# Attention without dividing the softmax: the sums go through DRAM into the gate, and three smaller moves

## The chip, the core and the metric

The kernel runs on one core of a Trainium2 chip. A core has TensorE (PE: matrix products, with a weight load, PEld, before each), VectorE (DVE), ScalarE (ACT) and GpSimd (POOL), which run their own instruction queues and wait for each other by semaphores, and SyncE (SP), which here only issues DMAs. Operands lie in on-chip memory of 128 partitions; products land in eight PSUM banks. The metric is the time on the device in microseconds, the median of several executions. Everything is float32; a product in full precision is made of three products of values that are split into a rounded high part and a low rest ("fp32r").

## The reference

Two layers; the change lies in the token mixer of the first, a forgetting attention over 1024 positions, 16 heads of 64:

```
proj = h @ w_in
q, k, v, o, fl = jnp.split(proj, [D, 2 * D, 3 * D, 4 * D], axis=-1)
q = rmsnorm(q.reshape(B, S, H, Dh), q_gain)
k = rmsnorm(k.reshape(B, S, H, Dh), k_gain)
logf = jax.nn.log_sigmoid((fl + b_f).astype(jnp.float32))
F = jnp.cumsum(logf, axis=1).transpose(0, 2, 1)
...
    logits = jnp.einsum('bqhd,bkhd->bhqk', q[:, q0:q1], k[:, :q1]).astype(jnp.float32) * scale
    decay = F[:, :, q0:q1, None] - F[:, :, None, :q1]
    logits = jnp.where(kpos <= qpos, logits + decay, -jnp.inf)
    p = jax.nn.softmax(logits, axis=-1).astype(v.dtype)
    outs.append(jnp.einsum('bhqk,bkhd->bqhd', p, v[:, :q1]))
att = jnp.concatenate(outs, axis=1).reshape(B, S, D)
return (att * jax.nn.sigmoid(o)) @ w_out
```

Before it stand `h = modulate(rmsnorm(x, norm1_g), shift, scale)` and the conditioning that gives shift and scale; after it a gated MLP with a convolution, then a second layer with a spatial-gating MLP and another gated MLP. The division in the softmax is by one number per query and head, so it may be made before the product with v, after it, or on the gate sigmoid(o), which the product is multiplied with.

## The kernel before

**Order.** The kernel is traced in the order of its code. A planner then draws the order of each engine at build time from a simulated timeline: an instruction that was traced earlier goes first, but one whose inputs are ready in that simulation may pass one that waits. SP's queue is ordered in the same way. In the attention part only a few orders are fixed by hand (`chain`); TensorE's order there is the planner's. A buffer ring hands a buffer out again when all that used it is done.

**Start (`fox`, L445 to L502).** Eight tiles of x are loaded; `square` sums each row on ScalarE, `rstd` makes the factors with some thirteen small operations on VectorE, for the tiles 0 and 1, 2 and 3, 4 to 7 together. `ada_first(q)` (L413) makes a quarter of shift and scale from two pieces of weights of 1 MB, multiplied and added on VectorE (L429, L431). `raw_pieces` (L403) says in which buffers the eight pieces lie: qq, w, kh, kl, w, pt, qq, w; the ring w has two slots, and qq, kh and kl are the buffers that hold q and k later. `norm_t` normalizes (L465), transposes on TensorE (L157) and copies to h (L471); the loop after it applies scale and shift on ScalarE (L492), rounds (L493) and subtracts (L119). The weights of the first three gate products (`o_weights(…, True)`, buffers qkv) are rounded on ScalarE (L126), and their low parts are made on POOL (L119).

**Gate products.** `o_proj(p)` computes o for a head pair, and `o_out` stores its sigmoid to the DRAM tile nso. Pairs 0 to 2 are computed at the start, pairs 3 to 7 in a loop with `o_proj` and a conditioning job each, after the projection of pair 0 (`proj`) and `forget`, which makes the sums F (fq on chip, nf in DRAM).

**Attention.** Eight head pairs p. `proj(p)` (matmuls pj) makes q, k and v of a pair in two halves of 512 positions, normalizes q and k per head (L590 to L598), and is the filler: `tick` lets some of its matmuls follow each score tile. `heads_qk(rw, half)` transposes q and k of a half (ps qk, L157), scales and rounds them on ScalarE into qq and kh (L697), makes the low parts on VectorE (L699) and copies kh once more (L703). The rows of kl that belong to the other head are zero; POOL writes them once (L686), 16 instructions. `scores(p, fb, qt)` does the query tile qt of 128 for both heads: POOL makes the decay row F[t]-F[s] and masks it (L738, L742), TensorE the products s, VectorE adds the two and takes the minimum (L762), ScalarE the exponent with its sum (L773), VectorE the reciprocal of the sum (L775); then the row is scaled by it, for head 0 on ScalarE (L777), for head 1 on VectorE (L779). `values(p, g, hd, v)` takes 256 queries g of one head: transposes of the probabilities (ms, L157), a copy (L797) and a low part (L119 pt), products pv with v; at the end the two halves of the product are added to av, and after head 1 VectorE multiplies the gate with it (L816), so, which was loaded from nso; the result goes to nat in DRAM (L818), for pair 7 to the chip. The output product (op) of the last stage reads nat and w_out.

The loop over pairs traces: value product of the last pair, v, `scores` 1, the end of this pair's projection (`until`), `heads_qk` of half 1, `scores` 2, value product (0, head 0), `scores` 3, value product (0, head 1), the second half of v, `scores` 4, and so on; near its end it prepares half 0 of the next pair. For pair 0 half 0 is prepared at L981, right before `scores` 0. Score tiles 0 to 3 need half 0 alone.

Of the kernel before, what the change touches and what calls it, by code (L numbers as in the profile page):

```python
# [8 lines left out]
F32 = mybir.dt.float32  # L9
# [58 lines left out]
class Trunk:  # L68
# [278 lines left out]
    def fox(self):  # L347
# [4 lines left out]
        nso = self.tile(self.dram, [8, P, S], F32, "nso")  # L352
        nf = self.tile(self.dram, [H, S], F32, "nf")
        self.xd = self.tile(self.dram, [4, 2, P, S], F32, "xd")
        h = {}
        c = self.const

        with ExitStack() as es:
# [44 lines left out]
            def raw_pieces():  # L403

                nm = ("qq", "w", "kh", "kl", "w", "pt", "qq", "w")[len(pieces)]
                pieces.append(nm)
                if nm == "pt":
                    return [T([P, 2, 2, 256], F32, "pt", 3) for _ in range(2)]
                return [self.wslot([P, 4, 2, 256], F32) if nm == "w" else T([P, 4, 2, 256], F32, nm, 1)]

# [41 lines left out]
            rs = []  # L452
            for st0, n in ((0, 2), (2, 2), (4, 4)):
                ss = self.tile(self.small, [P, 4], F32, "n_ss")
                for i in range(n):
                    j = self.square(ss, i, xn[st0 + i], self.hslot(F32).rearrange("p a f -> p (a f)"))
                    if st0 + i == 0:
                        self.chain("act", j)
                r = self.rstd(ss, n)
                rs += [r[:, i : i + 1] for i in range(n)]  # L460
# [223 lines left out]
            for hd in range(2):  # L684
                for c in range(0, S, P):
                    nc.gpsimd.tensor_scalar(  # L686
                        KL[hd][own[1 - hd], c : c + P], self.ones[own[1 - hd]], 0.0, None, op0=ALU.mult
                    )

# [41 lines left out]
            def scores(p, fb, qt):  # L731
# [22 lines left out]
                for j, (c0, c1) in enumerate(zip(cuts, cuts[1:])):  # L754
# [10 lines left out]
                    tick(n / P)  # L765
                    flush()
                for hd in range(2):
                    d = st_t[hd, qt][:, :nk]
                    nm = sm[hd][:, 0:1]
                    if nk > 512:  # L770
                        nc.vector.tensor_tensor(nm, nm, sm[hd][:, 1:2], op=ALU.min)
                    l = self.tile(self.small, [P, 1], F32, "ll")
                    nc.scalar.activation(d, d, AF.Exp, bias=nm, scale=-1.0, accum_out=l)  # L773
                    r = self.tile(self.small, [P, 1], F32, "lr")
                    nc.vector.reciprocal(r, l)  # L775
                    if hd == 0:
                        nc.scalar.activation(d, d, AF.Copy, scale=r)  # L777
                    else:
                        nc.vector.tensor_scalar(d, d, r, None, op0=ALU.mult)  # L779

            def values(p, g, hd, v):

                if hd == 0:
# [6 lines left out]
                for kt in range(0, 2 * g + 2, 2):  # L790
                    last = kt == 2 * g
                    blocks = [(kt, 2 * g), (kt, 2 * g + 1)]
                    blocks += [(kt + 1, 2 * g + 1)] if last else [(kt + 1, 2 * g), (kt + 1, 2 * g + 1)]
                    nb = len(blocks) * P
                    ps = self.transpose4([st_t[hd, qt][:, j * P : (j + 1) * P] for j, qt in blocks])
                    pt = T([P, 2, 512], F32R, "pt", 3)
# [45 lines left out]
            for p in range(PO, 8):  # L842
                o_proj(p)
                self.run_jobs(jobs, 1, u4)


# [133 lines left out]
            fb = f_rows(0)  # L980
            heads_qk(rws[0], 0)  # L981
            scores(0, fb, 0)
            v0 = None
            for p in range(8):
# [5 lines left out]
                until(p, 1)  # L990
                heads_qk(rws[p], 1)
                scores(p, fb, 2)
                values(p, 0, 0, v)
                scores(p, fb, 3)
                values(p, 0, 1, v)
# [1000 lines left out]
```

## Time and profile before

| | |
|---|---|
| median of 3 runs | 2636.36 us (2635.47 to 2638.59) |
| the profiled execution | 2637.63 us; its span 2635.8 |
| mean granted clock of TensorE | 0.988 |
| TensorE busy | 2552.9 us, 97% of the span |
| VectorE, ScalarE busy | 2074.0 us (79%), 1461.9 us (55%) |
| POOL busy | 183.7 us, all before 720 us |
| TensorE's chain that ended last | 86% of the span |

The span runs from the first to the last instruction. A row of the timeline gives the start, the duration, engine, line, operation, tiles (out<-in), shapes and, in brackets, the idle time before it and what ended it; ACTq or SPq is an engine's queue, which here issues DMAs. "PE s L104 <- ACT kh L703" means that a matmul of the scores waited for ScalarE's copy of kh at L703. PEclk is the share of full speed that TensorE was granted. Most matmuls are recorded under the helper's L104, transposes under L157, rounding under L126 and low parts under L119, so their tiles tell them apart: o (gate), pj (projection), s (scores), pv (values), op (output), ms (transposes and small sums).

### The profile page before, as it was taken

Reading aid. Unit: us, or ns where it says so; the run is one execution under the profiler, and the core shown is the slowest. Engines: PE = TensorE matmul, PEld = TensorE weight load, DVE = VectorE, ACT = ScalarE, POOL = GpSimd, SP = SyncE. Lnnn points to the kernel's source line nnn. Section 1 sums busy time; section 2 is a strip of 40 time slices with the busy share of each in tenths; the row PEclk is TensorE's granted clock in tenths of the full one; section 3 lists DMA queues with packets and bytes.
Section 4 is the critical chain, followed back from the end, with each engine's and each line's share of the span. In section 5 each row is a group of like instructions: output and inputs, shape, how many; then the busy total and the mean of one; then the engine's idle time right before and its main releaser. Section 6 shows DMA issues by size and latency. Waiting matters only on the chain.

```text
span 2635.8 us, 35388 instructions
## 1 busy us (share of the span) xinstructions
PE 2552.9 (97%) x12578; PEld 2176.1 (83%) x12578; DVE 2074.0 (79%) x3577; ACT 1461.9 (55%) x2313; POOL 183.7 (7%) x305
## 2 busy tenths in 40 slices
PE   5999999999999999999999999999999999999997
PEld 4988999998788888888887888888877888888886
DVE  7578788888668998898778776676888988886875
ACT  5337777777655545545446644554466555555444
POOL 3113222322200000000000000000000000000000
PEclk8999999999999999999999999999999999999999
DMA  7661111113242353557554256557451443328462
GB/s 230 200 232 53 57 57 57 57 53 113 84 129 68 124 168 128 158 160 275 184 185 150 93 161 191 189 189 271 156 191 50 133 130 128 116 96 295 159 198 90
DMA packets 316521, 379.46 MB, mean 144 GB/s; under 512 B 18872, under 2 KB 196152, under 8 KB 316344
## 3 DMA queue, kind: packets, MB, share of 16 engines
q1 hardware_dynamic: 316120, 377.14, 43.9%
q8 instruction: 99, 1.62, 0.2%
q14 instruction: 78, 0.64, 0.1%
q10 hardware_dynamic: 224, 0.06, 0.0%
HBM read 287.41 MB, written 89.72 MB: 143 GB/s over the span
## 4 chain that ended last, share of the span: by engine, by line
PE 86%; DVE 6%; ACT 3%; DMA 2%; issue 2%; SPq 0%; DVEq 0%; ACTq 0%
PE bankX L104 21%; PE banka L104 19%; PE bankY L104 18%; PE pj L104 9%; PE ms L104 5%; PE o L104 3%; PE ms L157 3%; PE s L104 2%; PE op L104 2%; PE pv L104 2%; PE ms L1818 1%; DVE ow L1149 1%; PE ms L281 1%; PE qk L157 1%; DVE x L1149 1%
## 5 line engine op out<-in xcount | busy, mean ns | idle before, releaser
L1136 ACT CAST ow<-rw 128x1024 fp32r<-128x1024 f32 (+1 forms) x438 | 398.0, 910 | 455.5 <-PE bankX L104 160.4
L1149 DVE TENSOR_TENSOR ow<-rw,ow 128x1024 fp32r<-128x1024 f32 (+1 forms) x438 | 456.7, 1045 | 148.3 <-ACT ow L1136 147.7
L104 PE MATMUL bankX<-hc,ow 128*128 128x512 f32 x1968 | 477.5, 391 | 1.1 <-DVE x L1149 1.0
L104 PEld LDWEIGHTS bankX<-hc,ow 128*128 128x128 f32 x1968 | 367.6, 188 | 78.8 <-DVE x L1149 1.8
L104 PE MATMUL banka<-hc,ow 128*128 128x512 f32 x1704 | 415.8, 393 | 0.8 <-DVE x L1149 0.8
L104 PEld LDWEIGHTS banka<-hc,ow 128*128 128x128 f32 x1704 | 319.6, 189 | 68.2 <-DVE x L1149 1.1
L104 PE MATMUL bankY<-hc,ow 128*128 128x512 f32 x1440 | 349.6, 391 | 0.0
L104 PE MATMUL pj<-x,h 128*128 128x384 f32 (+1 forms) x1536 | 315.0, 345 | 1.1 <-DVE smx L762 0.5
L104 PEld LDWEIGHTS bankY<-hc,ow 128*128 128x128 f32 x1440 | 269.2, 188 | 55.7 <-issue 0.5
L104 PEld LDWEIGHTS pj<-x,h 128*128 128x128 f32 x1536 | 267.7, 190 | 5.8 <-DVE smx L762 1.3
L1691 DVE SCALAR_TENSOR_TENSOR x<-x,prm,x 128x1022 f32<-128x1022 f32 (+1 forms) x160 | 204.0, 1279 | 2.9 <-ACT x L1689 2.3
L104 PE MATMUL bankY<-ow 128*128 128x512 f32 x720 | 203.5, 390 | 0.5 <-DVE x L1153 0.5
L104 PE MATMUL banka<-ow 128*128 128x512 f32 x672 | 187.4, 391 | 1.9 <-DVE x L1153 1.9
L104 PEld LDWEIGHTS bankY<-ow 128*128 128x128 f32 x720 | 134.7, 188 | 29.4 <-DVE x L1153 1.7
L104 PE MATMUL bankX<-ow 128*128 128x512 f32 x588 | 155.6, 390 | 0.1
L104 PEld LDWEIGHTS banka<-ow 128*128 128x128 f32 x672 | 125.7, 188 | 29.1 <-ACT x L1186 2.0
L104 PE MATMUL ms<-ow 128*128 128x512 f32 x546 | 140.0, 390 | 0.9 <-DVE pp L1149 0.9
L104 PE MATMUL pv<-pt,w 128*128 128x256 f32 (+1 forms) x640 | 122.3, 292 | 12.0 <-ACT pt L797 8.6
L104 PEld LDWEIGHTS bankX<-ow 128*128 128x128 f32 x588 | 110.2, 188 | 23.8 <-DVE ow L1149 0.5
L119 DVE TENSOR_TENSOR pt<-ms,pt 128x512 fp32r<-128x512 f32 (+1 forms) x160 | 100.4, 632 | 28.2 <-ACT pt L797 26.7
L104 PEld LDWEIGHTS ms<-ow 128*128 128x128 f32 x546 | 102.0, 188 | 23.7 <-DVE pp L1149 2.9
L104 PEld LDWEIGHTS pv<-pt,w 128*128 128x128 f32 x640 | 96.5, 191 | 20.2 <-ACT pt L797 12.9
(302 smaller groups left out, 3859.5 us busy)
## 6 DMA issues: line engine op xcount, KB each, us to landing
rw<-yd SPq DMA_DIRECT2D x210, 256.0 KB
rw<-in_ffn_w_up_dram SPq DMA_DIRECT2D x88, 512.0 KB
yd<-pp SPq DMA_DIRECT2D x60, 512.0 KB
rw<-in_ada_w_dram SPq DMA_DIRECT2D x48, 512.0 KB
rw<-in_ffn_w_down_dram SPq DMA_DIRECT2D x88, 256.0 KB
rw<-in_sgu_w_in_dram SPq DMA_DIRECT2D x32, 512.0 KB
yd<-x SPq DMA_DIRECT2D x30, 512.0 KB
fraw<-in_fox_w_in_dram SPq DMA_DIRECT2D x96, 128.0 KB
```

The costliest lines, as they stand in the source:

```text
L104: i = self.nc.tensor.matmul(out, lhsT, rhs, start=start, stop=stop, skip_group_check=self.strict)
L119: return (eng or self.nc.vector).tensor_tensor(lo, full, hi.bitcast(F32), op=ALU.subtract)
L157: i = self.nc.tensor.transpose(ps[: s.shape[1], j * P : (j + 1) * P], s, self.ident)
L281: i = nc.tensor.matmul(ps[:, j : j + 1], acc[:, j * P : (j + 1) * P], self.ones[:, 0:1], start=True, stop=True)
L1136: return self.ao(self.nc.scalar.copy(t[:, 0], src))
L1149: return self.vo(self.nc.vector.tensor_tensor(out, a, b, op=op))
L1691: self.vo(stt(o[:, j:], a[:, : S - j], w[2 - j], o[:, j:], op0=ALU.mult, op1=ALU.add))
L1818: k = nc.tensor.matmul(px[:, b * P : (b + 1) * P], vn[:, b, c * P : (c + 1) * P], sg[:, 0], start=True, stop=True)
```

## The change

Five parts. The sum of the exponents is no longer divided out in `scores`; the reciprocals of both heads go as one 128x2 store to a DRAM tile nl, and `values` loads them as two rows, each broadcast over 64 partitions, and multiplies the gate with them on POOL. Half 0 of pair 0 is prepared in the loop of the gate products, between pair 6 and pair 7. Half 1 of each pair is prepared one score tile and one value product later. The zeros of kl are written by ScalarE. The first norm makes its factors in five groups, and the weight pieces 5, 6 and 7 lie in w, w and pt in place of pt, qq and w.

```diff
+        nl = self.tile(self.dram, [H, S], F32, "nl")
...
-                nm = ("qq", "w", "kh", "kl", "w", "pt", "qq", "w")[len(pieces)]
-                pieces.append(nm)
-                if nm == "pt":
-                    return [T([P, 2, 2, 256], F32, "pt", 3) for _ in range(2)]
-                return [self.wslot([P, 4, 2, 256], F32) if nm == "w" else T([P, 4, 2, 256], F32, nm, 1)]
+                pieces.append(0)
+                if len(pieces) < 6:
+                    nm = ("qq", "w", "kh", "kl", "w")[len(pieces) - 1]
+                    return [self.wslot([P, 4, 2, 256], F32) if nm == "w" else T([P, 4, 2, 256], F32, nm, 1)]
+                if len(pieces) % 4:
+                    return [self.wslot([P, 4, 2, 256], F32)]
+                return [T([P, 2, 2, 256], F32, "pt", 3) for _ in range(2)]
...
-            for st0, n in ((0, 2), (2, 2), (4, 4)):
+            for st0, n in ((0, 2), (2, 1), (3, 1), (4, 2), (6, 2)):
...
-                    nc.gpsimd.tensor_scalar(
-                        KL[hd][own[1 - hd], c : c + P], self.ones[own[1 - hd]], 0.0, None, op0=ALU.mult
-                    )
+                    nc.scalar.activation(KL[hd][own[1 - hd], c : c + P], self.ones[own[1 - hd]], AF.Copy, scale=0.0)
...
+                l = self.tile(self.small, [P, 2], F32, "ll")
                 for hd in range(2):
                     d = st_t[hd, qt][:, :nk]
                     nm = sm[hd][:, 0:1]
                     if nk > 512:
                         nc.vector.tensor_tensor(nm, nm, sm[hd][:, 1:2], op=ALU.min)
-                    l = self.tile(self.small, [P, 1], F32, "ll")
-                    nc.scalar.activation(d, d, AF.Exp, bias=nm, scale=-1.0, accum_out=l)
-                    r = self.tile(self.small, [P, 1], F32, "lr")
-                    nc.vector.reciprocal(r, l)
-                    if hd == 0:
-                        nc.scalar.activation(d, d, AF.Copy, scale=r)
-                    else:
-                        nc.vector.tensor_scalar(d, d, r, None, op0=ALU.mult)
+                    nc.scalar.activation(d, d, AF.Exp, bias=nm, scale=-1.0, accum_out=l[:, hd : hd + 1])
+                r = self.tile(self.small, [P, 2], F32, "lr")
+                nc.vector.reciprocal(r, l)
+                nc.sync.dma_start(nl[2 * p : 2 * p + 2, qt * P : (qt + 1) * P].rearrange("h s -> s h"), r)
...
                     nb = len(blocks) * P
+                    if hd == 1 and kt == 0:
+                        rl = self.tile(self.tm, [P, 512], F32, "tm")[:, :256]
+                        for i in range(2):
+                            nc.sync.dma_start(
+                                rl[own[i]], nl[2 * p + i, g * 256 : (g + 1) * 256].partition_broadcast(DH)
+                            )
+                        nc.gpsimd.tensor_tensor(so, so, rl, op=ALU.mult)
...
             for p in range(PO, 8):
                 o_proj(p)
                 self.run_jobs(jobs, 1, u4)
+                if p == 6:
+                    heads_qk(rws[0], 0)
...
-            heads_qk(rws[0], 0)
             scores(0, fb, 0)
...
                 until(p, 1)
-                heads_qk(rws[p], 1)
                 scores(p, fb, 2)
                 values(p, 0, 0, v)
+                heads_qk(rws[p], 1)
                 scores(p, fb, 3)
                 values(p, 0, 1, v)
```

## The prediction

> **What bounds the kernel now.** I read the busy time by stage first, then TensorE's waits, then the single rows at the longest of them. The stages are cut where the work changes: loads and first norm (0 to 50), the first gate products (50 to 62), gate products and the first projection (62 to 180), attention (180 to 660), its output product (660 to 780), and everything behind it.
>
> ```profile
> span 2635.8 us, 35388 instructions
> ...
> core 0: us, PE busy (x) PEld busy (x) DVE busy (x) ACT busy (x) POOL busy (x), PEclk, DMA share, GB/s
> 0.00:50.00 50.00, 25.69 (x120) 20.62 (x121) 39.03 (x86) 31.34 (x55) 18.19 (x29) 0.83 0.91 290
> 50.00:62.00 12.00, 7.31 (x21) 5.47 (x20) 11.05 (x18) 5.99 (x10) 2.06 (x2) 0.72 0.21 54
> 62.00:180.00 118.00, 118.00 (x590) 104.32 (x590) 75.88 (x160) 37.73 (x71) 15.72 (x30) 1.00 0.71 233
> 180.00:660.00 480.00, 457.87 (x2909) 435.44 (x2909) 396.51 (x1142) 355.10 (x723) 134.46 (x224) 0.98 0.21 63
> 660.00:780.00 120.00, 111.83 (x625) 94.70 (x624) 77.41 (x179) 71.77 (x135) 13.22 (x22) 0.97 0.31 102
> 780.00:2636.00 1856.00, 1832.22 (x8321) 1515.57 (x8319) 1474.07 (x1996) 959.99 (x1322) 0.00 (x0) 1.00 0.48 159
> ```
>
> The columns are the stretch, its length, the busy time of each engine, the granted clock, and the DMA share. From 62 to 180 TensorE never idles; from 780 on it is 98.7% busy and the change touches nothing there. In attention it idles 480 - 457.9 = 22.1 us of 480, in the output product 8.2 of 120. The change takes no matmul away, so **all that it can win is idle time of TensorE before 780, and the half clock that follows idle time**. A count of instructions saved on VectorE or ScalarE is worth nothing by itself: they are busy 83% and 74% in attention, behind TensorE's 95%. These are TensorE's waits in attention, then two from the output product (total us, times, longest):
>
> ```profile
> PE pv L104 <- ACT pt L797: 7.2, 10, 2.1
> PE s L104 <- ACT kh L703: 4.7, 2, 3.5
> PE qk L157 <- DVE qkv L598: 3.5, 4, 1.7
> PE pv L104 <- DVE pt L119: 2.8, 6, 0.7
> PE ms L157 <- DVE pt L119: 2.0, 6, 0.4
> ...
> PE pv L104 <- ACT pt L797: 1.4, 2, 0.9
> PE ms L157 <- DVE pt L119: 1.4, 2, 0.7
> ```
>
> **The head preparation moved forward (first call, L981).** Now the first scores are traced right behind the preparation of their q and k. The rows at that place, and the clock after it:
>
> ```profile
> 189.19 1.28 ACT L773 ACT_TABLE_LOAD   x1
> ...
> 191.00 0.62 ACT L703 CAST kh<-kh 64x512 fp32r<-64x512 f32 x1
> ...
> 191.67 0.48 PE L104 MATMUL s<-kh,qq 128*128 128x128 f32 x1 [3.54 <-ACT kh L703]
> ...
> 192.00:198.00 6.00, 6.00 (x25) 5.90 (x25) 4.30 (x17) 4.86 (x13) 0.98 (x2) 0.51 0.00 0
> ```
>
> TensorE stands 3.54 us, because the last copy of k queues on ScalarE behind the exponent's table load. Then six busy microseconds run at 0.51 of the clock, which costs 6 x 0.49 = 2.9. With the preparation between the last two gate products (62 to 180, ScalarE busy 38 of 118 us), 6.4 us have no cause left. What is late next is the same table load: the last sigmoid must precede it, the first exponent follow it. It can uncover up to its 1.28. I take **-6** (bounds -6.4 to 0).
>
> **The second half of q and k moved back.** It now follows the score tile 2 and the first value product instead of standing before both; its data are needed by score tile 4, so nothing is due sooner.
>
> ```profile
> 263.01 1.33 PE L157 MATMUL qk<-ident,qkv 128*128 128x128 f32 x5 [1.70 <-DVE qkv L598]
> ...
> 263.00:267.00 4.00, 3.99 (x18) 3.99 (x19) 3.57 (x11) 2.61 (x4) 1.25 (x4) 0.60 0.12 36
> ```
>
> The four waits for the normalized q and k (3.5 in all) come at this place, and the longest is followed by 4 us at 0.60, worth 1.6. Together 5.1; the eight copies and subtractions of the move go on costing ScalarE and VectorE the same and could now stand before score tile 3. I take **-4** (bounds -5.1 to 0).
>
> **The division by the sum.** It leaves ScalarE for head 0, VectorE for head 1, and the reciprocals become half as many. The busy sums over 180 to 780 of the lines 777 (head 0), 779 (head 1) and 775 (reciprocal), then one place where it stands in the way:
>
> ```profile
> sum 600.00, ACT 49.70; mean ACT 24.85
> ...
> sum 600.00, DVE 36.15; mean DVE 18.07
> ...
> sum 600.00, DVE 19.79; mean DVE 9.89
> ...
> 638.14 1.15 ACT L777 ACTIVATE raw<-raw,lr 128x1024 f32<-128x1024 f32 x1
> ...
> 645.05 0.58 PE L104 MATMUL pv<-pt,w 128*128 128x256 f32 x1 [2.10 <-ACT pt L797]
> ...
> 645.00:649.00 4.00, 3.94 (x20) 3.76 (x21) 3.91 (x9) 3.88 (x8) 0.68 (x2) 0.57 0.20 72
> ```
>
> ScalarE loses 49.7 of 426.9 busy us (12%), VectorE 36.2 + 9.9 = 46 of 474 (10%; half the 19.8 of reciprocals stays). Also the way from exponent to transpose is shorter by a reciprocal and a scaling. The addressable waits: pv and ms 7.2 + 2.8 + 2.0 = 12.0 in attention, 2.8 behind it, the second kh wait 4.7 - 3.5 = 1.2, and the clock after the 2.10 us wait, 4 x 0.43 = 1.7: 17.7 us. They sit where ScalarE and VectorE have a backlog (two rows above, a 1.15 us scaling is 7 us ahead of the late copy in ScalarE's queue), so a tenth less work removes more than a tenth of them; but the projection's copies and splits that make the backlog all remain. Between 0 and 17.7 I take half, **-9**.
>
> **What it adds.** Per head pair and query tile one store of 256 single floats; per head pair and 256 queries, two broadcast loads and a POOL product of 128x256. Nothing of this feeds TensorE until L816 multiplies gate and output. No row shows a store of scattered floats or this product. All ends are bounded here by rows:
>
> ```profile
> q1 hardware_dynamic: 316120, 377.14, 43.9%
> ...
> 46.63 5.43 POOL L119 TENSOR_TENSOR x<-qkv,x 128x512 fp32r<-128x512 f32 x4
> ...
> 636.40 1.14 ACT L773 ACTIVATE cv<-cv,smx 128x1024 f32<-128x1024 f32 x1
> ...
> 647.22 0.41 DVE so L816
> ...
> 649.99 2.70 DMA fraw<-nat
> ...
> 247.84 2.31 DMA fraw<-in_fox_w_in_dram
> ```
>
> A mean packet takes 0.439 x 2635.8 x 16 / 316120 = 0.059 us, so 256 of them on 16 engines 0.94 us; 64 stores are 60 us of DMA time over 540, beside a share of 0.21. Zero to 0.94 each, hidden either way. The way through DRAM: from the end of a DVE result at 647.63 to its data back on chip at 652.69 are 5.1 us. The POOL product is half of 5.43/4, so 0.7. In all 5.8 us; the tightest distance from the last exponent of a pair (ends 637.54) to its last L816 (647.22) is 9.7. So it hides, with 3.9 us to spare. SP holds each store until its reciprocal and each load until its store; behind them wait the weight loads of the next pair, and those are not early: the last row is one that stands in the chain that ended last. A store that SP reaches before its reciprocal is ready delays them by that time. POOL holds the product until the load; behind it wait the bias rows (L738) of later scores, and behind these VectorE's L762. The POOL work is 32 x 0.7 = 22 us.
>
> In the Trainium skill, "SBUF — State Buffer", section "Who interferes with whom", VectorE and GpSimd share one port pair, and a GpSimd instruction that reads SBUF fully blocks a VectorE instruction with two SBUF inputs. The trace agrees: the three VectorE operations at 45.88, in the rows of the start below, take 7.52 where three like them at 35.67 take 2.33, while POOL runs its four splits. By that rule up to 22 of the 46 us saved on VectorE come back, and the term for the division would be nearer -5 than -9. "DMA: Bandwidth & Descriptors", section "Rules for kernel authors", says that a strided last dimension becomes one descriptor per element and tells us to avoid it; that speaks against this store, and the sum by it is the 0.94 us each already taken as the upper end.
>
> New small waits, from an order that the planner draws afresh and from SP's holds: by the waits of 0.2 to 0.7 that stand all over attention I take **+2** (bounds 0 to +10).
>
> **The start (0 to 62).** Three edits. The zeroing of kl moves from POOL to ScalarE; the first norm is cut into five groups; three of the eight pieces of the first conditioning weights get other buffers.
>
> ```profile
> 35.40 11.25 POOL L686 TENSOR_SCALAR kl<-ones 64x128 fp32r<-64x128 f32 x16 [7.95 <-DVE tm L431]
> ...
> 45.88 7.52 DVE L431 SCALAR_TENSOR_TENSOR tm<-qq,cact,tm 128x512 f32<-128x512 f32 x3
> ...
> 54.90 0.68 DVE L119 TENSOR_TENSOR h<-h,h 128x512 fp32r<-128x512 f32 x1
> ...
> 55.64 4.63 PE L104 MATMUL o<-h,x 128*128 128x512 f32 x10 [4.69 <-DVE h L119]
> ...
> 12.46 0.16 DVE L148 TENSOR_TENSOR rs_t<-rs_y 128x2 f32<-128x2 f32 x1
> ...
> 35.30 2.01 SPq L424 DMA_DIRECT2D qq<-in_ada_w_dram  x2
> 35.67 2.33 DVE L431 SCALAR_TENSOR_TENSOR tm<-w,cact,tm 128x512 f32<-128x512 f32 x3
> ```
>
> The four POOL splits (46.63, shown above) wait behind the zeroing, then hold VectorE up for some 5 us, and TensorE stands 4.69 us at 55.64. Without the zeroing they come about 4 us earlier and hold VectorE up there instead, while it is just as full: so nothing sure is won, at best the 4.69 and the slow clock of 50 to 62 (7.31 x 0.28 = 2.0). Against it: 16 zeroings on ScalarE at 0.2 to 0.4 each, at most 6.4, which the idle 6 us of 50 to 62 and the 80 of 62 to 180 hide; uncovered they delay h by that much. Two more groups of the norm add 22 small operations x 0.16 = 3.5 us to VectorE, which has 11 us idle in the first 50. The seventh piece goes to a slot that is read until 38.0, and was issued at 35.30: 2.7 us later, though its data are first used at 43.6. I take **-2** (bounds -7 to +6).
>
> **Sum.** -6 - 4 - 9 + 2 - 2 = -19. The profiled execution took 2637.6, its span and 1.8 around it; 2637.6 - 19 = 2618.6. The median of the runs is 1.3 lower than that execution, so I forecast **2617**.
>
> **The rivals.**
> 1. *The waits are only renamed.* TensorE goes on standing for VectorE at other instructions, since the projection's work that makes the backlog is untouched; the moved preparation gives some of its win back before score tile 3. For it: VectorE keeps 90% of its work and POOL takes port time. Against it: the 3.54 us wait has no successor of its size. It leaves 0 to -9: around 2631. Chance 0.20.
> 2. *The sums come late.* At the end of each pair L816 waits for the POOL product, that for the load, that for SP, which stands before a weight load whose buffer is not free. It decides once the 5.8 us grow beyond 9.7, that is with 4 us of SP queueing. Then VectorE stands, with the splits of pt behind it, and TensorE with them: 8 pairs x (3 us and 1.6 of clock) = 37 on top of -19, about 2654. Against it: other pairs have more distance, and loads are planned far ahead. Chance 0.10.
> 3. *All of it comes true.* -6.4 - 5.1 - 17.7 - 5 = -34: 2602. Speaks for it that each short wait has ScalarE or VectorE as its releaser; against it, that the planner has made the order for its own estimates and not for the chip. Chance 0.10.
>
> That the division isn't removed is ruled out by the diff.
>
> **How the numbers follow.** The forecast has 0.60, with its own range 2606 to 2628. About 0.2% (5 us) is what a measurement of this kernel can tell from no change, so faster means under 2631. Faster: 0.60 + 0.10 + nearly half of rival 1 = 0.79. Same: the rest of rival 1 and a mild rival 2, 0.13. Slower: 0.08. The range 2602 to 2636 takes in the third and first rivals and leaves out the second and the outermost ends.
>
> **What would show it.** Right: no wait over 1 us on kh near 185, and a clock of 1.00 from 190 to 198; no waits qk <- qkv; lines 777 and 779 gone, pv <- pt under 5 us; idle TensorE from 180 to 660 under 12 us; L816 waits for nothing. Wrong: VectorE waiting for POOL at L816, POOL's L738 waiting for a DMA into tm, L762 waiting for POOL, SP standing on the store. The start is judged by when TensorE begins its unbroken run, now at 55.6; if that moves by more than 6 us either way, or if the time behind 780 changes by more than 3 us, my account has missed something.

## The result, and the profile after

| | before | after |
|---|---|---|
| median of 4 runs each | 2635.91 us | 2804.61 us (2799.38 to 2808.62) |
| after to before | | 1.0634, 95% interval 1.0612 to 1.0656 |
| the profiled execution; its span | 2637.63; 2635.8 | 2807.48; 2805.7 |
| mean granted clock of TensorE | 0.988 | 0.960 |

The change costs 169 us, where 19 were to be won. First the stretches of after, cut as before (length, busy time of PE, PEld, DVE, ACT and POOL, granted clock, DMA share, GB/s); the output product now ends at about 950, so that the fourth stretch begins at 960:

```profile
core 0: us, PE busy (x) PEld busy (x) DVE busy (x) ACT busy (x) POOL busy (x), PEclk, DMA share, GB/s
180.00:660.00 480.00, 390.57 (x2295) 367.56 (x2294) 278.95 (x804) 239.55 (x508) 111.19 (x198) 0.89 0.33 46
660.00:780.00 120.00, 88.19 (x504) 82.65 (x503) 66.38 (x173) 60.97 (x125) 23.73 (x41) 0.83 0.46 73
780.00:960.00 180.00, 143.39 (x717) 119.37 (x717) 94.96 (x212) 80.17 (x152) 21.14 (x35) 0.87 0.41 94
960.00:2805.00 1845.00, 1822.85 (x8284) 1508.25 (x8282) 1462.37 (x1981) 952.39 (x1312) 0.00 (x0) 1.00 0.49 158
```

From 960 on TensorE is busy 98.8% of the time, as it was behind 780 before: nothing is lost there. From 180 to 960 it idles 89.4 + 31.8 + 36.6 = 157.8 us, against 22.1 + 8.2 in the same work before, and runs at 0.83 to 0.89 of its clock. Every engine has less to do per microsecond, so none of them is the bound. The waits from 180 to 960 (total us, times, longest) say who stands for whom:

```profile
POOL so L801 <- DMA tm<-nl: 369.2, 27, 50.9
DVE cv L763 <- POOL cv L739: 47.9, 10, 9.2
PE pv L104 <- ACT pt L804: 30.0, 15, 8.9
PE pj L104 <- ACT x L126: 26.3, 6, 8.1
PE s L104 <- DVE smx L763: 21.6, 6, 7.6
SPq L798 <- DMA nl<-lr: 220.7, 32, 9.7
```

Read from the first row: POOL's new product waits for the loads of the reciprocals; behind it in POOL's queue stand the bias rows (L739), for these VectorE's addition (L763), and for that TensorE. SP itself stands 221 us for its own stores to nl. One such place in the chain that ended last (start, length, what):

```profile
277.61 8.01 DMA nat<-so
...
285.68 0.33 SPq L785
...
286.11 7.45 DMA nl<-lr
...
293.62 0.45 SPq L798
...
294.12 2.69 DMA tm<-nl
...
297.06 0.11 POOL so L801
...
297.77 1.02 POOL raw L739
...
298.82 0.69 DVE raw L763
```

A store of 1 KB takes 7.45 us until SP knows that it has landed (8.5 in the median of 62 such stores). The load behind it takes 2.69, then the product, the bias row and the addition follow one another. The same place in POOL's timeline, idle time in brackets:

```profile
297.06 0.73 POOL L801 TENSOR_TENSOR so<-so,tm 128x256 f32<-128x256 f32 x1 [14.92 <-DMA tm<-nl]
297.77 1.01 POOL L739 TENSOR_SCALAR raw<-fb,fq 128x896 f32<-128x896 f32 x1
```

And the DMA engines at this place: the window 286 to 294 with its busy share in 40 slices of 0.2 us, then the packets of 290 to 293 alone:

```profile
DMA  0002456800001000000000000000000000000000
...
DMA packets 417, 0.15 MB, mean 19 GB/s; under 512 B 288, under 2 KB 416, under 8 KB 416
...
DMA packets 0, 0.00 MB, mean 0 GB/s; under 512 B 0, under 2 KB 0, under 8 KB 0
```

The store was issued at 286.1, and all packets, the 256 small ones with them, are through before 289. For the three microseconds of the second window nothing moves at all, and the store has still not landed (293.56): it is not the engines' time that makes it long.

### The profile page after: what moved, and what is told of

Read it like the earlier page. It is cut to its first block, busy times and chain, and to the rows that moved or that the text cites. A ratio compares the mean times of both kernels' runs of the same rounds, so it can differ in the third digit from the quotient of the medians.

```text
span 2805.7 us, 35596 instructions
## 1 busy us (share of the span) xinstructions
PE 2603.5 (93%) x12578; PEld 2215.5 (79%) x12578; DVE 2031.8 (72%) x3469; ACT 1420.1 (51%) x2265; POOL 183.8 (7%) x321
## 4 chain that ended last, share of the span: by engine, by line
PE 75%; DMA 12%; DVE 6%; issue 3%; ACT 3%; SPq 1%; POOL 1%; DVEq 0%; POOLq 0%; ACTq 0%
PE bankX L104 20%; PE banka L104 18%; PE bankY L104 17%; PE pj L104 5%; PE ms L104 5%; DMA nl<-lr 3%; PE o L104 3%; PE ms L157 2%; DMA nat<-so 2%; PE s L104 1%; PE op L104 1%; DMA tm<-nl 1%; DMA fraw<-in_fox_w_in_dram 1%; DMA fraw<-nat 1%; PE pv L104 1%
## 5 line engine op out<-in xcount | busy, mean ns | idle before, releaser
L104 PE MATMUL pj<-x,h 128*128 128x384 f32 (+1 forms) x1536 | 333.9, 360 | 46.0 <-ACT x L126 26.3
L104 PEld LDWEIGHTS pj<-x,h 128*128 128x128 f32 x1536 | 285.1, 201 | 54.7 <-ACT x L126 27.8
L104 PE MATMUL pv<-pt,w 128*128 128x256 f32 (+1 forms) x640 | 130.0, 308 | 48.2 <-ACT pt L804 30.0
L104 PEld LDWEIGHTS pv<-pt,w 128*128 128x128 f32 x640 | 103.9, 205 | 59.0 <-ACT pt L804 35.2
L763 DVE CUSTOM_DVE_ANT_0 cv<-s,cv 128x512 f32<-128x512 f32 (+3 forms) x109 | 60.1, 556 | 109.4 <-POOL cv L739 47.9
```

The source lines that it names most:

```text
L104: i = self.nc.tensor.matmul(out, lhsT, rhs, start=start, stop=stop, skip_group_check=self.strict)
L763: nc.vector.tensor_tensor_reduce(d, pss[hd][:, :n], d, -1.0, 3.4e38, ALU.add, ALU.min, sm[hd][:, j : j + 1])
```

## The experiments

The planner draws the orders afresh for each kernel, so a few microseconds between two of them may be its doing. "Before" is run beside each group of them, at 2636.3 to 2639.9 us. The medians are of 4 to 10 executions, those of e3 and e8 of 2.

### Which part loses

**e1** puts the division back and keeps the four other parts; **e2** leaves the division out altogether; **e3** has the stores and nobody who reads them; **e4** has loads and product and no stores.

```diff
 e1: scores as in before; nl, its loads and the POOL product gone
 e2: after without these, the scores undivided
-                r = self.tile(self.small, [P, 2], F32, "lr")
-                nc.vector.reciprocal(r, l)
-                nc.sync.dma_start(nl[2 * p : 2 * p + 2, qt * P : (qt + 1) * P].rearrange("h s -> s h"), r)
...
-                        nc.gpsimd.tensor_tensor(so, so, rl, op=ALU.mult)
 e3: after without the loads and the product
 e4: after without the reciprocals and the stores, nl written once
+        nc.sync.dma_start(nl.rearrange("h (t s) -> (h t) s", s=P), self.ones)
```

> The changed kernel with the division put back where it was (reciprocal and scaling of both heads in the score step) and without the store of the sums, the loads and the POOL product; the moved preparation of q and k, the zeroing on ScalarE, the norm groups and the weight buffers stay as changed. Every theory puts the loss into the sums' way through DRAM, so this one should be faster than before: by the prediction's terms -6 (first half of q and k), -4 (second half) and -2 (start), about 2624 us; the trace of the changed kernel already shows the start and the first scores some 11 us earlier, so 2620 to 2628. If it is slower than before, the loss lies in the order of the moved work and all theories on the sums fall.

> The changed kernel with the division left out altogether: no reciprocals, no store, no loads, no POOL product; the output isn't divided by the sums. It is the bound of what undividing the softmax can win. By the prediction's term for the division (-9, bounds 0 to -17.7) it takes 9 us less than the run with the division put back, about 2615 us. If it is still over 2700, the loss is not in the sums' way through DRAM.

> The changed kernel with the reciprocals and the 64 stores, but without the loads and the POOL product; the output isn't divided. Theory A (a store of 256 single floats takes about 7.4 us until it is confirmed, and whatever SP issued behind it is confirmed no sooner): the loads of weights and of gates and the stores of results behind it stay late, and at least 60 of the 168 us lost remain, 2680 or more. Theory B (the loss is the chain of waits in order: SP stands for the store's landing before each load, POOL stands for the load with the bias rows of the next scores behind it): nobody waits for a store now, so within 15 us of the run without division, about 2615 to 2630.

> The changed kernel with the loads and the POOL product, but without reciprocals and stores; the sums' rows in DRAM are filled once at the start with ones, so the output isn't divided. Theory A and theory B both expect almost no loss against the run without division: a load takes about 2.7 us and nothing precedes it, 2612 to 2630. Theory C (the POOL product itself, 0.73 us each in POOL's queue and on the port it shares with VectorE, does the harm): it stays slow, 2680 or more.

| | us | to before, 95% |
|---|---|---|
| e1 | 2627.10 | 0.9958 (0.9943 to 0.9973) |
| e2 | 2641.67 | 1.0019 (1.0009 to 1.0029) |
| e3 | 2684.05 | 1.0176 (1.0155 to 1.0197) |
| e4 | 2646.68 | 1.0036 (1.0022 to 1.0049) |

e1 wins 10.5 us: the four other parts are not to blame. But e2 was a puzzle: it only leaves work out of e1, and is 14.6 us slower. The groups of one stretch far behind attention (1000 to 1200) show where; the row of e2, then that of e1:

```profile
L104 PE MATMUL bankX<-hc,ow 128*128 128x512 f32 x360 | 89.7, 398 | 0.7 <-DVE x L1146 0.7
```

```profile
L104 PE MATMUL bankX<-hc,ow 128*128 128x512 f32 x366 | 88.8, 391 | 0.2 <-DVE x L1151 0.2
```

The same matmul takes 398 ns in place of 391, in a part that the edit doesn't touch. e2 and e4 are the two kernels without the small tile lr, and without it all that is allocated behind it lies elsewhere on chip. So both were made again with the reciprocals computed and unused, **e5** and **e6**.

```diff
 e5: as e2, e6: as e4, but with
+                r = self.tile(self.small, [P, 2], F32, "lr")
+                nc.vector.reciprocal(r, l)
```

> The run without division once more, but with the reciprocals computed (and used by nobody), so that their tile stays allocated and everything behind it in on-chip memory keeps its address. The output isn't divided. In the first such run, which had no tile lr, attention and output product ended 12 us earlier than with the division put back, yet the run was 14.6 us longer: its 512-column matmuls behind 780 us took 398 ns instead of 391. Theory (addresses): the shift of the following tiles by the missing small tile made them slower; here they take 391 again and the total is some 11 us below the run with the division put back, 2614 to 2619. Rival (the undivided exponents or the new order slow the later stages): it stays at 2635 or more.

> The loads and the POOL product without the stores, as before, but with the reciprocals computed so that the addresses stay; the sums' rows in DRAM hold ones, so the output isn't divided. By the difference of the first two such runs (5 us) the loads and the product cost 5 us over the run without division: 2618 to 2625.

e5 took 2618.99 us (0.9941, 0.9924 to 0.9957), e6 2616.82 (0.9932, 0.9917 to 0.9947), and the row in e5 is back at 391:

```profile
L104 PE MATMUL bankX<-hc,ow 128*128 128x512 f32 x360 | 87.3, 391 | 0.2 <-DVE x L1148 0.2
```

Those 22.7 us (2641.67 - 2618.99) are not the change's, and without them the parts add up. Leaving the division out is worth 2627.1 - 2619.0 = 8.1 us by the medians. Loads and product on top of that cost nothing (-2.2). **The stores alone, with nobody waiting for their data, cost 2684.1 - 2619.0 = 65 us**, and the whole change another 120.

### What makes a store slow

**e8** issues the stores from ScalarE's queue. **e7** turns the reciprocals into rows on TensorE first, two of 1 KB for each 256 queries, and keeps loads, product and waits.

```diff
 e8
-                nc.sync.dma_start(nl[2 * p : 2 * p + 2, qt * P : (qt + 1) * P].rearrange("h s -> s h"), r)
+                nc.scalar.dma_start(nl[2 * p : 2 * p + 2, qt * P : (qt + 1) * P].rearrange("h s -> s h"), r)
 e7, in values, head 0
+                    ps = self.transpose4([lr[2 * g], lr[2 * g + 1]])
+                    nc.scalar.copy(rl[:2, 256:], ps[:2, :256])
+                    nc.sync.dma_start(nl[2 * p : 2 * p + 2, g * 256 : (g + 1) * 256], rl[:2, 256:])
```

> The whole computation, but the reciprocals of 256 queries are transposed on TensorE, copied to two rows on chip and stored as two runs of 1 KB, in place of two stores of 256 single floats each; the loads, the POOL product and all waits in order stay. Theory A+B as the runs so far have it (SP's and POOL's waits in order lose much only because a store of single floats takes 7.4 us to be confirmed): the round trip falls to about 5 us, the loss goes nearly whole, 2618 to 2640. Theory B alone (any store that is waited for in order costs this): it stays over 2700.

> The changed kernel with its store of single floats issued from ScalarE's queue instead of SP's, all else alike. If the store harms others by standing ahead of them in SP's own ring, weight loads, gates and results on SP are confirmed in their old time and only SP's waits for the sums' landing remain: 2700 to 2760. If the memory takes 7 us to confirm it whatever the ring, and later transfers of the same DMA engines are confirmed after it in any ring, nothing is won: 2790 or more, and ScalarE now waits for the reciprocals as well.

e8: 2756.10 us (1.0457, 1.0436 to 1.0479), 48 less than after and still 120 over before: another queue is not the cure. By its time alone e8 lies in the range of its first theory; the landings below show that the mechanism of the second is at work all the same. Where the 48 us come from was not tried. e7: 2638.82 (1.0000, 0.9988 to 1.0011), so with long rows 166 us go, though each load still waits for its store. Why it is not as good as e5 was not tried; its waits from 180 to 960 point at its transposes, which stand in TensorE's order ahead of those of the probabilities (the first row is 5.3 from 180 to 660 in e5 and 21.2 in e7):

```profile
PE pv L104 <- ACT pt L807: 22.6, 17, 3.8
PE ms L157 <- DVE lr L777: 5.1, 4, 1.4
```

Small pieces, then; but are they slow because they are many, or because they share the place that they are written to? **e9** and **e13** store the same 256 floats, each 512 B or 64 B from the next; **e10** writes 128 pieces of 8 B into 1 KB. All three are e3 otherwise.

```diff
 e9 (e13 with 16 in place of 128)
-        nl = self.tile(self.dram, [H, S], F32, "nl")
+        nl = self.tile(self.dram, [H, S, 128], F32, "nl")
...
+                nc.sync.dma_start(nl[2 * p : 2 * p + 2, qt * P : (qt + 1) * P, 0].rearrange("h s -> s h"), r)
 e10
+        nl = self.tile(self.dram, [8, S, 2], F32, "nl")
...
+                nc.sync.dma_start(nl[p, qt * P : (qt + 1) * P], r)
```

> The stores alone, as in e3 (loads and product left out, so the output lacks the division by the sums), but each of the 256 floats of a store goes to a place of its own, 512 B from the next. What makes a store's confirmation take 7 to 8 us though its packets have passed in 1 us? Theory L (shared places): 128 floats fall into one row of 512 B, and writes into the same place are carried out one after another. Then here the median time from issue to landing falls to 2 to 4 us and the kernel takes 2619 to 2635 us, near e5 (2619.0). Theory N (number): 256 writes cost what 256 writes cost, wherever they go. Then landing stays at 7 to 8 us and the kernel at 2675 to 2695 us, like e3 (2684.1).

> The stores alone again (loads and product left out), but the scratch is laid out query by query, so that a store is 128 writes of 8 B into one stretch of 1 KB, in place of 256 writes of 4 B into two of 512 B. Theory L (shared places): as many bytes in as few places, the landing is halved at most by the pieces being fewer within each place, and if the place alone counts it stays at 7 to 8 us with the kernel near e3 (2684.1). Theory N (number): half the writes, so 3.5 to 4.5 us to landing, and the kernel between e5 and e3, 2635 to 2660 us.

> The stores alone, as e9, but each float 64 B from the next in place of 512 B (loads and product left out). How large is the place that writes share? If it is 64 B or less, the kernel takes 2612 to 2625 us as e9 (2617.9) and the chain's landings stay near 1.5 us. If it is 512 B, 8 floats share one and the kernel lies between e9 and e10 (2631.5), 2620 to 2640 us with landings of 2.5 to 4 us.

| | writes of a store | writes into each 64 B | landing: median, shortest | us | to before, 95% |
|---|---|---|---|---|---|
| e3 | 256 of 4 B | 16 | 8.5, 7.1 | 2684.05 | 1.0176 (1.0155 to 1.0197) |
| e10 | 128 of 8 B | 8 | 3.5, 2.6 | 2631.54 | 0.9976 (0.9966 to 0.9986) |
| e9 | 256 of 4 B | 1 | 1.7, 1.5 | 2617.92 | 0.9922 (0.9900 to 0.9943) |
| e13 | 256 of 4 B | 1 | 1.6, 1.5 | 2613.95 | 0.9912 (0.9895 to 0.9928) |

The landing is the time in us from a store's issue to the last of the sixteen steps that the trace shows on its semaphore, taken over 63 stores of each run from 180 to 780 us. As many writes, each to a place of its own, cost nothing: **it is the sharing.** e9 and e13 agree to 0.01 us in the shortest landing, though e13 puts 8 floats into each 512 B and e9 one; so sharing 512 B costs nothing by itself, and nothing here speaks for a place of more than 64 B.

How the price grows with the writes into a place is open. e10 came out below both of its theories in time, and its landing was as the theory of numbers had it; half as many writes, of double size, take 1.9 us more than e13's, where e3's take 6.8 more. Nor do the runs show why a shared place is slow, and places below 64 B were not tried.

Why does e3 lose 65 us with nobody reading nl? Transfers that have nothing to do with the store are late, too. Rows of the chains, e3 first, then e13:

```profile
293.77 10.75 DMA fb<-nf
...
315.09 9.18 DMA fraw<-in_fox_w_in_dram
```

```profile
290.53 3.21 DMA fb<-nf
...
362.37 2.93 DMA fraw<-in_fox_w_in_dram
```

The loads of fb and of weights (fraw) take 10.75 and 9.18 us in place of 3.21 and 2.93. Counted over e3 from 180 to 780, the 40 weight loads that were issued while a store to nl was out landed after 9.3 us in the median, and each of them behind that store; 25 others took 2.3. In e8 the stores go through ScalarE's queue and the weight loads through SP's, and it is the same (180 to 960): 28 loads issued while a store was out took 8.9 us in the median, each landing behind the store, and 38 others 2.6. Two of the 28:

```profile
241.49 9.43 DMA fraw<-in_fox_w_in_dram
...
322.49 8.82 DMA fraw<-in_fox_w_in_dram
```

The Trainium skill, "DMA: Bandwidth & Descriptors", section "Queues, rings and completion order", says that a DMA's semaphore increment lands only after every earlier write from the same DMA engine, across its queues. The trace agrees, by these counts of e3 and e8.

Late landings hold SP up as well: it loads a gate into a buffer (so) only when the result that was stored from there has landed. Its waits for that from 180 to 960, in e3 and then in e5:

```profile
SPq L785 <- DMA nat<-so: 141.2, 25, 11.5
```

```profile
SPq L783 <- DMA nat<-so: 36.7, 25, 3.2
```

The page of the Trainium skill named above, "DMA: Bandwidth & Descriptors", section "Specifications", has transfers below 512 B done by reading, modifying and writing; e13 shows that 4 B pieces by themselves cost nothing measurable here.

### Who stands for the store

The other 120 us (e3 to after). **e12** lets the loads read a second scratch that is written once, so that they wait for no store. **e14** and **e15** (this one with e12's loads) move the product from POOL to VectorE, traced ahead of the product with av; **e16** and **e17** (this one with e12's loads) do the same, but behind that product and on its result.

```diff
 e12
-                                rl[own[i]], nl[2 * p + i, g * 256 : (g + 1) * 256].partition_broadcast(DH)
+                                rl[own[i]], n1[2 * p + i, g * 256 : (g + 1) * 256].partition_broadcast(DH)
 e14, e15
-                        nc.gpsimd.tensor_tensor(so, so, rl, op=ALU.mult)
...
+                                nc.vector.tensor_tensor(so, so, rl, op=ALU.mult)
                                 nc.vector.tensor_tensor(so, so, av, op=ALU.mult)
 e16, e17
                                 nc.vector.tensor_tensor(so, so, av, op=ALU.mult)
+                                nc.vector.tensor_tensor(so, so, rl, op=ALU.mult)
```

> After, but the loads read another scratch (filled with ones once at the start, so the output lacks the division by the sums) and no longer wait for the stores; stores, loads and product are all there. What makes after (2804.6) 120 us slower than the stores alone (e3, 2684.1)? Theory W (waits in order): the load waits for the store's landing at the head of SP's queue and the product for the load on POOL, each with other work behind it. Then here the loads are out at once and the kernel takes 2675 to 2715 us; the little over e3 is that loads issued behind a store are confirmed late, too. Theory C (the loads and the stores get in each other's way in the memory, or there is too much on the queue): 2770 us or more.

> The whole computation: after, with only the product of gate and reciprocals taken off POOL; VectorE does it in the output's last product, right ahead of the product with av. Stores, loads and the dependence stay. e12 cut the dependence and kept 75 of the 120 us over e3 (2684.1), its POOL standing 207 us for the gate loads. Theory Q (POOL's queue): the product, early in POOL's order, makes the bias rows behind it wait for whatever load is confirmed late, so without it most of 120 us goes: 2690 to 2725 us. Theory S (SP's queue): SP standing for the store's landing holds the later loads back; that is unchanged, and the kernel stays above 2755 us.

> Both at once: the loads read the scratch filled with ones and wait for no store (the output lacks the division by the sums), and the product is VectorE's, late. Theory Q: nothing is left in POOL's or SP's order that waits for a store, so the kernel is at e3 (2684.1) and a little: 2680 to 2705 us, and e14 to e15 is the price of SP's waits. If it stays near e12 (2759.6), the 75 us belong to the additional transfers behind slow stores, not to any queue of an engine.

> The whole computation, as e14, but VectorE multiplies by the reciprocals behind the product with av, on its result, so that it can't be issued early (in e14 it stood 17 us ahead of that product in VectorE's order, and VectorE stood 235 us for the loads). Theory Q (the price is that of the queue of the engine that stands for a late load): nothing stands early on POOL or VectorE now, so the kernel comes down to 2690 to 2740 us, below after (2804.6). Theory S (SP's standing for the store's landing, and what is issued behind it late): above 2780 us.

> As e16, with the loads reading the scratch of ones, so that they wait for no store (the output lacks the division by the sums). Theory Q: 2680 to 2705 us, near the stores alone (e3, 2684.1). Theory T (the loads behind slow stores cost as transfers, whoever waits): 2740 us or more, as e12 (2759.6).

| the product | loads wait for the stores | loads wait for none |
|---|---|---|
| on POOL, early | after: 2804.61 | e12: 2759.63 (1.0474, 1.0443 to 1.0505) |
| on VectorE, early | e14: 2862.18 (1.0852, 1.0834 to 1.0871) | e15: 2804.94 (1.0644, 1.0617 to 1.0671) |
| on VectorE, last | e16: 2737.35 (1.0375, 1.0357 to 1.0394) | e17: 2686.24 (1.0181, 1.0149 to 1.0213) |

e12 came out between the two theories. Without the dependence 75 us stayed, and POOL's waits from 180 to 960 name their cause: the product now stands for the gate's load, which a slow store in front of it makes late.

```profile
POOL so L803 <- DMA so<-nso: 207.3, 18, 21.8
```

e14 and e15 came out slower than any theory had expected: e14 lies above 2755, as theory S said, but also above after, and e15 is 45 us over e12. The timeline of e14 shows that the edit hadn't done what it was for: the planner put the product with the reciprocals 3 us ahead of the other, and VectorE, which has far more behind it than POOL, stood there.

```profile
323.51 0.43 DVE L823 TENSOR_TENSOR so<-so,tm 128x256 f32<-128x256 f32 x1 [7.45 <-DMA tm<-nl]
...
326.57 0.41 DVE L824 TENSOR_TENSOR so<-so,av 128x256 f32<-128x256 f32 x1
```

```profile
DVE so L823 <- DMA tm<-nl: 234.6, 30, 14.1
```

Put where it can't be issued early, the same product on the same engine costs 125 us less (e16), and without the dependence it is at e3 (e17: 2.2 us over it). What is left in e16 stands in SP's queue, while VectorE hardly waits:

```profile
DVE so L824 <- DMA tm<-nl: 8.6, 3, 4.5
...
SPq L798 <- DMA nl<-lr: 228.8, 34, 10.9
```

So the loss falls into steps, each with a pair of kernels: e5 to e3, +65: stores that are slow to land make other transfers late. e3 to e17, +2: the further loads and a late product. e17 to e16, +51: SP stands for each store before it issues the load, and all that it would issue next is late. e16 to after, +67: POOL stands early for the load, with the bias rows behind it. Together +185.6, on a kernel (e5) that is 17 us under before's 2635.9; the result is +168.7. By the other path, through e12, the last two steps come to +73 (e17 to e12, the product's place) and +45 (e12 to after, the dependence), so their sizes hold to some 6 us.

### A version that beats both

**e11** computes everything. VectorE transposes the reciprocals in blocks of 32 by 32, and a store is 16 pieces of 128 B. Loads, the product on POOL and all waits are as in after.

```diff
-                nc.vector.reciprocal(r, l)
-                nc.sync.dma_start(nl[2 * p : 2 * p + 2, qt * P : (qt + 1) * P].rearrange("h s -> s h"), r)
+                if qt % 2 == 0:
+                    r = lr[qt // 2] = self.tile(self.tm, [P, 512], F32, "tm")
+                    nc.gpsimd.memset(r[:, :P], 0.0)
...
+                nc.vector.reciprocal(r[:, qt % 2 * 32 : P : 64], l)
+                if qt % 2:
+                    nc.vector.transpose(r[:, P:256], r[:, :P])
+                    nc.sync.dma_start(
+                        nl[p, qt // 2].rearrange("(k b s) -> b k s", b=4, s=32),
+                        r[0:P:32, P:256].rearrange("b (k s) -> b k s", s=32),
+                    )
```

> The whole computation. The reciprocals of two query tiles are turned into rows on VectorE (a transposition in blocks of 32 by 32) and stored as 16 pieces of 128 B, one store for each group of 256 queries; loads, product and waits stay as after. If the 512 writes for each group were the cause, the round trip takes under 5 us, nobody waits for it, and the kernel comes out at e5 (2619.0) plus what 32 transpositions, 32 zero fills and 32 stores cost: 2616 to 2628 us, below e7 (2638.8), whose transpositions stood in TensorE's order. If the round trip through DRAM costs what it does by its in-order waits whatever the pieces, it stays above 2636 us.

2621.09 us, 0.9939 of before (0.9925 to 0.9954), and 183 us under after. It is within 2.1 us of e5, which divides by nothing; whether it also beats e1 (0.9958, 0.9943 to 0.9973) the intervals leave open. The groups from 180 to 780 show its price:

```profile
L783 DVE STREAM_TRANSPOSE tm<-tm 128x128 f32<-128x128 f32 x32 | 9.9, 309 | 0.7
...
L778 POOL MEMSET tm<- 128x128 f32 x30 | 6.1, 204 | 1.3
```

## Why the prediction was wrong

**The failing step is "What it adds", at its first bound.** A store of 256 single floats was priced by its packets, 0 to 0.94 us of DMA time, "hidden either way". The packets do pass that quickly, as the empty window in after shows. But a transfer has a second length, from issue to confirmed landing, and that was taken from a store of long rows: the 5.1 us for the way through DRAM. In after the store alone takes 7.45 and the load 2.69, 10.7 from one issue to the other's landing (286.11 to 296.81), which is past the 9.7 us that the prediction had to spare; the median of 62 stores is 8.5. No row of before had a store of this kind; the upper bound should not have been the price of its packets.

**The second rival was the right mechanism at the wrong place and price.** It let L816 wait at the end of each pair, 8 times, for 37 us, because SP stood before a weight load; what made the sums late was the landing of the store itself. What waits is the POOL product, traced at the first block of head 1 of each 256 queries and not at the last product; it stood 27 times for 369 us, and it holds the bias rows from the first group on. The prediction named these rows as the ones that queue behind it, and then counted only the tightest distance, the last of a pair. And what nobody's wait explains, the lateness of all transfers behind a store (65 us), was in no rival. It needs no reader of nl at all.

**The rest of the sum came out right, but not by all of its terms**, and the whole result hides both. e1 has the three of them that aren't the division, and its stretches, and then its waits from 180 to 660, answer to those of before:

```profile
50.00:62.00 12.00, 11.27 (x54) 9.10 (x53) 9.93 (x20) 7.58 (x13) 0.00 (x0) 1.00 0.39 94
...
180.00:660.00 480.00, 460.90 (x2944) 438.37 (x2943) 393.44 (x1133) 354.17 (x718) 131.20 (x221) 0.98 0.21 66
...
192.00:198.00 6.00, 6.00 (x39) 5.78 (x38) 4.57 (x17) 4.05 (x9) 1.20 (x2) 1.00 0.14 45
```

```profile
PE pv L104 <- ACT pt L798: 7.8, 9, 2.6
...
PE s L104 <- ACT kh L703: 3.1, 4, 1.2
```

The first matmul of the scores and the first one behind the output product (bankX) show where time was won; before, then e1, then e5:

```profile
187.80 0.22 PE L104 MATMUL s<-kh,qq 128*128 128x128 f32 x1
...
781.26 2.12 PE L104 MATMUL bankX<-h,h 128*128 128x512 f32 x8 [0.29 <-DVE x L1153]
```

```profile
176.75 0.31 PE L104 MATMUL s<-kh,qq 128*128 128x128 f32 x1
...
771.42 5.05 PE L104 MATMUL bankX<-h,h 128*128 128x512 f32 x21 [1.55 <-DVE x L1155]
```

```profile
176.79 0.31 PE L104 MATMUL s<-kh,qq 128*128 128x128 f32 x1
...
761.19 6.71 PE L104 MATMUL bankX<-h,h 128*128 128x512 f32 x21 [2.78 <-DVE x L1152]
```

- First and second half of the preparation, start and small waits: -6 - 4 - 2 + 2 = -10, measured -10.5 (e1). The sum is right by luck. e1 is 11.1 us ahead at its first score, some 2 of them because 12 of 216 matmuls of the projection come later. From 62 us to there TensorE idles in neither kernel, so this lead, about 9 us, is the start's, where -2 was forecast with -7 as the outer bound: from 50 to 62 TensorE is busy 11.27 us at 1.00, where it was 7.31 at 0.72. Which of the start's three edits did it was not tried.
- From the first score to bankX e1 takes 594.7 us and before 593.5, so both halves of the preparation, with the small waits, brought about -1 in place of -8. What they aimed at did go: the clock from 192 to 198 is 1.00 where it was 0.51, the longest wait for kh is 1.2 where it was 3.54, and no wait of qk for qkv is left. But TensorE idles 30.3 us between the two rows, against 30.6: the waits went to other instructions, as the first rival said.
- The division: -9, measured -8.1 by the medians (e5 against e1), whose intervals overlap, and -10.3 between the two rows (594.7 to 584.4). This term came true. Its waits pv <- pt are 7.8 in e1, still there with the division back, and 5.3 in e5.
- The sum of -19 without the store: e5 measured 2638.06 - 2618.99 = 19.1, by the same luck in the parts. Two of the prediction's signs fail in e5 as well: TensorE idles 16.9 us from 180 to 660 where it should have been under 12, and pv <- pt is not under 5.
- The POOL product: 0.7, measured 0.73. The rule on the port that VectorE and GpSimd share (the Trainium skill, "SBUF — State Buffer", "Who interferes with whom") would have taken back up to 4 us of the division's term. Loads and product together cost nothing in e6 (-2.2 against e5), so in the time of the kernel these 22 us of POOL work don't show it. The rule is for two inputs in SBUF, and about 247 of VectorE's 367 busy us in e6 (180 to 660) take one from PSUM. The prediction's own row at 35.67, at full speed, ran beside POOL's zeroing, so its trace agreed for the splits alone.

So the number of the forecast would have held for the same idea with a store that lands quickly: e11 is at 2621.1, 4 us from the 2617 forecast.

## What to carry to other kernels

A DMA has two prices, the time of its packets and the time to its confirmed landing, and a small scattered store must be judged by the second; before writing a column of single floats into a row, make it a row on chip. A store that is slow to land delays what was issued behind it, whoever reads it, so "nobody waits for it" is no cover. An instruction that waits for such a transfer belongs behind the last thing in its engine's queue that doesn't need it: with one store and one product, its place in the queue alone made 125 us here.

## What the runs showed of the hardware that was not expected

- Many small writes into the same 64 B of DRAM land late, while the DMA engines stand empty: 256 writes of 4 B, 16 to each 64 B, after 8.5 us, the same writes 64 B apart after 1.6 (medians of e3, e13). They cost the kernel 65 us, and nothing 64 B or more apart.
- What is issued while such a store is out lands behind it, from another queue as well: weight loads took 8.9 us in e8 where others took 2.6 (medians).
- Without one small tile of a pool, matmuls of 512 columns far behind it took 398 ns in place of 391 and the kernel 22.7 us more (e2 against e5). That it goes with this tile is shown; that the addresses behind it are the cause is argued only, and which operand's address counts was not tried.
